# Reading the moving operand of 256-column products alternately from its two halves, in a hybrid encoder layer on one core

## The chip, the core and the metric

The kernel runs on one core of one Trainium2 chip. The metric is the device time of one execution in microseconds (us). Three runs of the kernel before took 881.15, 881.81 and 883.31 us, so its median is 881.81 us.

## The reference

One layer of a streaming encoder on x of 512 tokens by 1024 channels, all in float32:

```python
h = rms_norm(x, norm_mix)
proj = h @ w_in                      # 1024 -> 5*1024 + 3*1024
u_pool, u_lru, q, k, v, g_logits = split(proj)
gates = sigmoid(g_logits + b_gate)   # three gates of 1024 channels
y_pool = pool_mixer(u_pool)          # causal means over 2, 4, 8, 16 tokens, a 256x256 map per group
y_lru = rglru_mixer(u_lru)           # causal conv, two gates, a scan over tokens
y_sb = stick_breaking_attention(rms_norm(q), rms_norm(k), v)   # 8 heads of 128, causal
merged = sum(gates[b] * (y_b @ w_branch[b]) for b in range(3))
x = x + merged @ w_out
h2 = rms_norm(x, norm_ffn)
x = x + (silu(h2 @ w_ffn_gate) * (h2 @ w_ffn_up)) @ w_ffn_down   # 1024 -> 2816 -> 1024
```

## The kernel before, in words

Channels lie on the 128 partitions and tokens in the free dimension (512 of them), except for q, k and v, which are made with tokens on the partitions. To keep float32 accuracy on TensorE every operand is split into a high part of a reduced float32 type (`F32R`) and a low part that holds the rest: ScalarE (ACT) copies and rounds the high part, VectorE (DVE) subtracts to get the low part (`split_w`, lines 128 and 129, and `split_a`, lines 1425 and 1426). A product then takes three matmuls per block of k: high by high, high by low, low by high.

There are two kinds of products.

Products of 512 columns (`mm3`, lines 296 to 298, and lines 363, 721 and 818) stream all 512 tokens, or 512 weight columns. Their moving operand goes through `il`, which reads it alternately from its two halves: column 0, 256, 1, 257 and so on. Their results lie in PSUM in that order, and every reader undoes it with `in_order` (a step of two in PSUM) and `two` (the same shape of the unmixed tile). The attention products (z and py, also through `mm3`) do the same in blocks of 128 columns, of 64 and 64 (`b=64`); their widths are 128 x 4, 128 x 3 and 128 x 2.

Products of 256 columns come from the use of Strassen-like schemes: a 2 x 2 block product is made from seven products of sums of blocks instead of eight products, and each of the seven works on half of the tokens (`H` = 256 columns). One such product is 2 output blocks x 4 blocks of k x 3 matmuls, or 24 matmuls, each with its own load of 128 x 128 weights. There are four stages of them:

- the third branch's gate, two chunks of seven products (`product`, line 305; chunks at lines 873 to 901)
- the third branch's projection, 14 products in the order `BORDER` (line 1260)
- the feed-forward's gate and up projections, nine chunks of seven (`seven`, from line 1461, `product` again, line 305)
- the feed-forward's down projection, seven products of 20 blocks of k (`piece`, line 1633)

These read their moving operand straight through, 256 adjoining columns. Each product writes one half of a PSUM bank (`ps[:, w, half * H:(half + 1) * H]`). Partial sums are carried between banks by snapshots: after a product, ACT copies a half bank to SBUF (`act(t[:, :, ts_], src[:, :, ss], AF.Copy)`, lines 893, 1266 and 1477), and at the end of a chunk DVE adds the whole bank to it (`gate_done`, line 868; `merge7`, lines 1230 and 1232; `finish_act`, line 1452; `add`, line 1624, and line 1650 at the very end, which is followed by the store of the result).

The weights' split tiles rotate over three buffers each for high and low (`wp`). A buffer has room for 1024 + 128 elements, and a tile may begin at an offset in it. For the 256-column stages the first four products of a stage use offsets of 0, 4, 8 and 12 elements, and all later ones 16; all other weights begin at 0:

```python
OFF = 16
STEPS = (0, 4, 8, 12)
...
def weight_tiles(nh, nl, o=0):
    return [wp.tile([P, 1024 + 128], F32R, tag=tag, name=n)[:, o:o + 1024]
```

The order of the work on each engine is that of the program, with priorities (`tc.high_priority`) by which the splits of later weights are put ahead; background tasks are queued in `bg` and `abg` and called by `tick`. The weights come by DMA from the SP queue, and partly by adding DMAs from the GpSimd queue, which form the sums of blocks.

Of the kernel before, what the change touches and what calls it, by code (L numbers as in the profile page):

```python
# [32 lines left out]
H = S // 2  # L33
# [34 lines left out]
def layer_kernel(ctx: ExitStack, tc: tile.TileContext, x, xt, vecs, w_in, w_qkv7, w_gate7, w_pool, w_rg, w_ig,  # L68
# [38 lines left out]
    def two(ap, b=H):  # L107
        w = ap.ndim == 3
        if b == H:
            return ap.rearrange("p w (a b) -> p w a b" if w else "p (a b) -> p a b", b=b)  # L110
        return ap.rearrange("p (c a b) -> p c a b", a=2, b=b)

    def halves(t):
        return [t[:, 0:2, :], t[:, 2:4, :]]
# [185 lines left out]
    def product(a_, b_, ps, half, first, last, ws=(0, 1)):  # L300
        for w in ws:
            o = ps[:, w, half * H:(half + 1) * H]
            for k in range(4):
                for n, (a, b) in enumerate(((0, 0), (0, 1), (1, 0))):
                    nc.tensor.matmul(o, a_[a][:, w, k, :], b_[b][:, k, :],  # L305
                                     start=first and n == k == 0,
                                     stop=last and n == 2 and k == 3, skip_group_check=True)

# [117 lines left out]
    with ExitStack() as first:  # L426
# [438 lines left out]


        def gate_done(cc, j, t, ps):
            dve.tensor_tensor(t, t, ps, ALU.add)
            for w in range(2):
                act(t[:, w, :], t[:, w, :], AF.Sigmoid, scale=-1.0 if j else 1.0,  # L870
                    bias=vcol("b_gate", 16 + 2 * (2 * cc + w) + j))
            nc.gpsimd.dma_start(gd2[cc, j], t)

        for cc in range(2):
            tx, ty = b4([2, S], f"gx{cc}"), b4([2, S], f"gy{cc}")
            if cc:

                dve.memset(pb.tile([P, 2, S], F32, tag="mm", name="skip_g")[:, 0, 0:1], 0.0)
            Y = pb.tile([P, 2, S], F32, tag="mm", name=f"ps_gy{cc}")
            X = pb.tile([P, 2, S], F32, tag="mm", name=f"ps_gx{cc}")  # L880
            lo, hi = slice(0, H), slice(H, S)
            plan = {"11": (Y, 1, True, tx, lo, Y, hi),
                    "12": (X, 0, True, None, None, None, None),
                    "S2": (Y, 1, False, tx, hi, Y, hi),
                    "S1": (X, 1, False, ty, hi, X, hi),
                    "S3": (Y, 1, False, ty, lo, Y, hi),
                    "S4": (X, 1, False, None, None, None, None),
                    "22": (Y, 0, False, None, None, None, None)}
            for nm in ORDER:
                ps, half, first_, t, ts_, src, ss = plan[nm]  # L890
                product(weights("seven", 3 + cc, nm, 0), BQ[WITH[nm]], ps, half, first_, True)
                if t is not None:
                    act(t[:, :, ts_], src[:, :, ss], AF.Copy)
                if nm == "S4":
                    gate_done(cc, 0, tx, X)
                if nm == "22":
                    gate_done(cc, 1, ty, Y)
                tick(2)
                if (cc, nm) == (1, "12"):
                    q_scales()  # L900
# [305 lines left out]
    with ExitStack() as third:  # L1206
        ap2 = third.enter_context(tc.tile_pool(name="ap2", bufs=4, reuse_waits="tile"))
        bg.extend([lambda n=n: third_part(n) for n in range(4)] + [lambda n=n: fourth_part(n) for n in range(4)])
        gts = {}
        for u in range(2):  # L1210
            for i in range(2):
                gts[u, i] = ap2.tile([P, 2, S], F32, tag="g", name=f"g2{u}{i}")
                for j in range(2):
                    nc.sync.dma_start(gts[u, i][:, j, :], gd2[u, j][:, i, :])

        lo, hi = slice(0, H), slice(H, S)

        plan = {"11": ("Y", 1, True, 0, lo), "12": ("X", 0, False, None, None),
                "S1": ("X", 1, True, 1, hi), "S2": ("Y", 1, False, 0, hi),
                "S3": ("Y", 1, False, 1, lo), "S4": ("X", 1, False, None, None),  # L1220
                "22": ("Y", 0, False, None, None)}
        bank, snaps = {}, {}

        def merge7(u, i, ps):
            t, g, c = snaps[u, i], gts[u, i], 2 * u + i
            m = pairs[c]
            with tc.high_priority(60):
                if (u, i) in gated:
                    t = g
                    dve.tensor_tensor(t, g, ps, ALU.mult)  # L1230
                else:
                    dve.tensor_tensor(t, t, ps, ALU.add)
                    dve.tensor_tensor(t, t, g, ALU.mult)
                dve.tensor_tensor(m, m, t, ALU.subtract if i else ALU.add)
            h, l = corner([2, S], f"mth{c}", F32R), corner([2, S], f"mtl{c}", F32R)
            act(h, m, AF.Copy)
            dve.tensor_tensor(l, m, h.bitcast(F32), ALU.subtract)
            for j in range(2):
                mt[2 * c + j] = h[:, j, :], l[:, j, :]


        gated = [(0, 0), (0, 1), (1, 0)]

        def gate7(u, i):
            t, m = snaps[u, i], pairs[2 * u + i]
            dve.tensor_tensor(t, t, gts[u, i], ALU.mult)
            nc.gpsimd.dma_start(m, t, accum_op=ALU.add)

        for u, nm in BORDER:
            z, half, first_, sn, ts_ = plan[nm]  # L1250
            if (u, z) not in bank:
                bank[u, z] = fp.tile([P, 2, S], F32, tag="mm", name=f"ps_b{z}{u}")
            ps = bank[u, z]
            ah = weights("b7", u, nm)
            b = BH[nm]
            for w in range(2):
                o = ps[:, w, half * H:(half + 1) * H]
                for k in range(4):
                    for n, (x_, y_) in enumerate(((0, 0), (0, 1), (1, 0))):
                        nc.tensor.matmul(o, ah[x_][:, w, k, :], b[k][y_], start=first_ and n == k == 0,  # L1260
                                         stop=n == 2 and k == 3, skip_group_check=True)
            if sn is not None:
                if (u, sn) not in snaps:
                    snaps[u, sn] = ap2.tile([P, 2, S], F32, tag="t", name=f"bt{u}{sn}")
                with tc.high_priority(EARLY):
                    act(snaps[u, sn][:, :, ts_], ps[:, :, hi], AF.Copy,
                        scale=-1.0 if sn and (u, sn) in gated else 1.0)
            if nm in ("S2", "S3") and (u, sn) in gated:
                gate7(u, sn)
            tick()  # L1270
            if nm == "S4":
                merge7(u, 0, ps)
            if nm == "22":
                merge7(u, 1, ps)
# [3 lines left out]
    with ExitStack() as ffn:  # L1278
# [170 lines left out]

        def finish_act(t, ps, a):  # L1450

            dve.tensor_tensor(t, t, ps, ALU.add)
            act(t[:, 0, :], t[:, 0, :], AF.Silu)
            dve.tensor_tensor(a, t[:, 0, :], t[:, 1, :], ALU.mult)

# [3 lines left out]
        def seven(c):  # L1459
# [13 lines left out]
            for n, (nm, ps, half, first, t, ts_, src, ss) in enumerate(plan):  # L1473
                make_a(n0 + n + 3)
                product(A.pop((c, nm)), B[0, WITH[nm]], ps, half, first, True)
                if t is not None:
                    act(t[:, :, ts_], src[:, :, ss], AF.Copy)
                if c == DOWN - 1 and nm in PRE:
                    split_d2("11", PRE.index(nm), 0, 0)
                if nm == "S4":  # L1480
                    finish_act(tx, X, a[:, 0, :])
                if nm == "22":
                    finish_act(ty, Y, a[:, 1, :])
# [136 lines left out]
                "22": ("y", 0, True, [(1, lo, "y", lo)])}  # L1620

        def add(q, i, ts_, z, ss):
            t, ps = x1p[q, i][:, :, ts_], XY[q, z][:, :, ss]
            dve.tensor_tensor(t, t, ps, ALU.subtract if i else ALU.add)

        def piece(nm, q, use, ps, half, first, last, ws=(0, 1)):
            n, kh, k0, nk = use
            a_, b_ = DA[nm, n], DB[nm, kh]
            for w in ws:
                o = ps[:, w, half * H:(half + 1) * H]  # L1630
                for k in range(nk):
                    for i, (a, b) in enumerate(((0, 0), (0, 1), (1, 0))):
                        nc.tensor.matmul(o, a_[a][:, w, k0 + k, :], b_[b][:, k, :],  # L1633
                                         start=first and i == k == 0,
                                         stop=last and i == 2 and k == nk - 1, skip_group_check=True)

        for nm in DORDER:
# [3 lines left out]
            for q in range(2):  # L1641
                if (nm, q) == ("22", 1):

                    make_d(len(dsets))
                    for w, ps in enumerate((XY[1, "y"], XY[0, "x"])):
                        ws = slice(w, w + 1)
                        for p_, use in enumerate(USE[q]):
                            piece(nm, q, use, ps, half, first and p_ == 0, p_ == 2, (w,))
                        t = x1p[q, 1][:, ws, lo]
                        dve.tensor_tensor(t, t, ps[:, ws, lo], ALU.subtract)  # L1650
                        store(q, 1, lo, ws)
                    continue
                for p_, use in enumerate(USE[q]):
# [60 lines left out]
```

## Time and profile before

| | us |
|---|---|
| median of three runs | 881.81 |
| the profiled execution | 882.75 |
| its span, first to last instruction | 881.0 |
| TensorE matmul (PE) busy | 868.6 |
| TensorE weight load (PEld) busy | 798.1 |
| VectorE (DVE) busy | 740.9 |
| ScalarE (ACT) busy | 525.7 |
| GpSimd (POOL) busy | 90.9 |

The profile is that of one execution. Its span is a little shorter than the device time. An engine's busy time counts each moment once, though matmuls overlap: each is shown from its start to its modelled end, and the next starts before that. So the pace of PE is read from the starts, not from the durations. A row of a group gives line, engine, operation, what it writes and reads, shapes and count, then busy us and mean ns of one, then the idle time before it and what ended that. A row of the timeline gives start, duration, and in brackets the idle time before and its cause. The chain of work that ended last is followed back from the last instruction, at each step to what released it or to the instruction before it on its engine.

### The profile page before, as it was taken

The numbers are of one execution on the slowest core, as the hardware profiler recorded it, in microseconds if no ns is written. First come the engines' busy times: TensorE is split into PE (matmuls) and PEld (weight loads), VectorE is DVE, ScalarE is ACT, GpSimd is POOL, SyncE is SP. The second block draws the span as 40 slices with busy tenths as digits, with TensorE's granted clock in tenths as the row PEclk, the third lists the DMA queues.
The fourth block names the chain that finished last, engine by engine and source line by source line (L and its number), as shares of the span: only waits on it lengthen the run. The fifth ranks groups of instructions, "written<-read, shape, count | busy, mean of one in ns | idle before, by whom it ended". The sixth has DMA issues, their size and how long they took to land.

```text
span 881.0 us, 14269 instructions
## 1 busy us (share of the span) xinstructions
PE 868.6 (99%) x5563; PEld 798.1 (91%) x5563; DVE 740.9 (84%) x958; ACT 525.7 (60%) x730; POOL 90.9 (10%) x130
## 2 busy tenths in 40 slices
PE   9999989999999999999999999999999999999998
PEld 7888878888899888889889998889999999999998
DVE  7899787998786599977898786699988888899974
ACT  7555979556956556565664545464555555755642
POOL 1110002132433101000001100000000000121200
PEclk9999999999999999999999999999999999999999
DMA  9596346798592786735727855344533433798913
GB/s 338 151 306 187 96 159 174 200 330 259 179 277 72 226 252 198 221 121 154 230 84 171 188 168 175 103 141 134 163 99 96 119 99 119 225 238 204 188 31 120
DMA packets 116643, 154.08 MB, mean 175 GB/s; under 512 B 8160, under 2 KB 90080, under 8 KB 116576
## 3 DMA queue, kind: packets, MB, share of 16 engines
q1 hardware_dynamic: 103904, 107.30, 38.3%
q0 software_dynamic: 12528, 45.62, 21.7%
q8 instruction: 43, 0.70, 0.3%
q10 hardware_dynamic: 144, 0.26, 0.1%
q14 instruction: 24, 0.20, 0.1%
HBM read 132.71 MB, written 18.87 MB: 172 GB/s over the span
## 4 chain that ended last, share of the span: by engine, by line
PE 78%; DVE 11%; ACT 6%; DMA 2%; issue 2%; SPq 1%; ACTq 0%; DVEq 0%
PE ps_y L305 10%; PE ps_x L305 8%; PE ps_q L818 7%; PE ps_dy L1633 6%; PE ps_dx L1633 5%; DVE wlo L129 3%; PE ps_br L296 3%; PE ps_br L297 3%; PE ps_br L298 3%; PE ps_bY L1260 3%; PE ps_gate L721 2%; PE ps_gy L305 2%; PE ps_bX L1260 2%; PE ps_gx L305 2%; ACT whi L128 1%
## 5 line engine op out<-in xcount | busy, mean ns | idle before, releaser
L128 ACT ACTIVATE whi<-raw 128x1024 fp32r<-128x1024 f32 x69 | 72.8, 1055 | 80.1 <-PE ps_out L297 16.1
L129 DVE TENSOR_TENSOR wlo<-raw,whi 128x1024 fp32r<-128x1024 f32 x69 | 84.4, 1223 | 23.5 <-ACT whi L128 22.9
L129 DVE TENSOR_TENSOR wlo<-qw,whi 128x1024 fp32r<-128x1024 f32 x48 | 58.5, 1222 | 19.1 <-ACT whi L128 19.0
L128 ACT ACTIVATE whi<-qw 128x1024 fp32r<-128x1024 f32 x48 | 50.5, 1053 | 29.8 <-PE ps_q L818 14.8
L1425 ACT ACTIVATE wh_S<-w_S 128x1024 fp32r<-128x1024 f32 x36 | 38.2, 1065 | 34.9 <-PE ps_y L305 20.8
L1537 POOL DMA_DIRECT2D dw<-in_w_down_dram x20 | 16.9, 862 | 310.1 <-DMA dw<-in_w_down_dram 251.1
L1426 DVE TENSOR_TENSOR wl_S<-w_S,wh_S 128x1024 fp32r<-128x1024 f32 x36 | 43.8, 1222 | 4.5 <-ACT wh_S L1425 4.4
L1425 ACT ACTIVATE wh<-w 128x1024 fp32r<-128x1024 f32 x27 | 28.7, 1065 | 27.9 <-issue 9.3
L1426 DVE TENSOR_TENSOR wl<-w,wh 128x1024 fp32r<-128x1024 f32 x27 | 33.0, 1222 | 9.8 <-ACT wh L1425 9.8
L1425 ACT ACTIVATE whdS<-dw 128x1024 fp32r<-128x1024 f32 x20 | 21.3, 1065 | 22.5 <-PE ps_dy L1633 11.0
L1426 DVE TENSOR_TENSOR wldS<-dw,whdS 128x1024 fp32r<-128x1024 f32 x20 | 24.3, 1223 | 6.5 <-ACT whdS L1425 6.4
L1076 DVE TENSOR_TENSOR_SCAN E<-K,ahead 128x512 f32<-128x512 f32 (+3 forms) x32 | 25.4, 815 | 3.9 <-ACT K L1072 3.9
L298 PE MATMUL ps_gate<-HH,wlo 128*128 128x512 f32 x64 | 25.0, 390 | 2.2 <-DVE wlo L129 2.2
L296 PE MATMUL ps_br<-yHH,whi 128*128 128x512 f32 x64 | 24.6, 385 | 1.4 <-ACT up L963 1.4
L296 PE MATMUL ps_gate<-HH,whi 128*128 128x512 f32 x64 | 25.1, 392 | 0.0
L297 PE MATMUL ps_gate<-HL,whi 128*128 128x512 f32 x64 | 24.9, 389 | 0.0
L296 PE MATMUL ps_lru<-HH,whi 128*128 128x512 f32 x64 | 24.6, 384 | 0.0
L296 PE MATMUL ps_br<-yph,whi 128*128 128x512 f32 x64 | 24.5, 383 | 0.0
L296 PE MATMUL ps_pool<-HH,whi 128*128 128x512 f32 x64 | 24.5, 383 | 0.0
L297 PE MATMUL ps_lru<-HL,whi 128*128 128x512 f32 x64 | 24.3, 379 | 0.0
L298 PE MATMUL ps_lru<-HH,wlo 128*128 128x512 f32 x64 | 24.3, 379 | 0.0
L297 PE MATMUL ps_pool<-HL,whi 128*128 128x512 f32 x64 | 24.3, 379 | 0.0
(737 smaller groups left out, 3441.2 us busy)
## 6 DMA issues: line engine op xcount, KB each, us to landing
raw<-in_w_in_dram SPq DMA_DIRECT2D x31, 512.0 KB, 5.3
qw<-in_w_qkv_dram SPq DMA_DIRECT2D x24, 512.0 KB, 7.1
dw<-in_w_down_dram POOLq DMA_DIRECT2D x20, 512.0 KB, 7.4
w<-in_w_ffn_gate_dram SPq DMA_DIRECT2D x36, 256.0 KB, 3.5
w<-in_w_ffn_up_dram SPq DMA_DIRECT2D x36, 256.0 KB, 4.3
raw<-in_w_branch_dram SPq DMA_DIRECT2D x16, 512.0 KB, 4.0
qw<-in_w_qkv_dram POOLq DMA_DIRECT2D x12, 512.0 KB, 8.1
qd<-r POOLq DMA_DIRECT2D x12, 512.0 KB, 7.5
```

The source lines that it names most:

```text
L128: act(hi, raw, AF.Copy)
L129: dve.tensor_tensor(lo, raw, hi.bitcast(F32), ALU.subtract)
L296: nc.tensor.matmul(ps, lh, rh, start=start, stop=False, skip_group_check=skip)
L297: nc.tensor.matmul(ps, lh, rl, start=False, stop=False, skip_group_check=skip)
L298: nc.tensor.matmul(ps, ll, rh, start=False, stop=stop, skip_group_check=skip)
L305: nc.tensor.matmul(o, a_[a][:, w, k, :], b_[b][:, k, :], start=first and n == k == 0, stop=last and n == 2 and k == 3, skip_group_check=True)
L818: nc.tensor.matmul(ps[:, a, :], b_[:, k, ts_], il(a_[:, kk, :]), start=first and n == k == 0, stop=n == 2 and k == 3, skip_group_check=True)
L1076: dve.tensor_tensor_scan(E[:, c0:c0 + n][:, ::-1], K[:, c0 + 1:c0 + n + 1][:, ::-1], ahead[:, S - n:][:, ::-1], 0.0, ALU.mult, ALU.add)
L1260: nc.tensor.matmul(o, ah[x_][:, w, k, :], b[k][y_], start=first_ and n == k == 0, stop=n == 2 and k == 3, skip_group_check=True)
L1425: act(h, src, AF.Copy)
L1426: dve.tensor_tensor(l, src, h.bitcast(F32), ALU.subtract)
L1633: nc.tensor.matmul(o, a_[a][:, w, k0 + k, :], b_[b][:, k, :], start=first and i == k == 0, stop=last and i == 2 and k == nk - 1, skip_grou ...
```

## The change

The moving operand of the 256-column products goes through a new helper `il2`, which reads columns 0, 128, 1, 129 and so on. The bank's half then holds the tokens in that order, so all readers of these banks get `in_order2` on the PSUM side, a step of two inside each half, and `two2` on the SBUF side. The number of instructions, their sizes, the buffers, the offsets of the weights and the DMAs stay as they are.

```diff
+    def il2(ap):
+        return ap.rearrange("p (a b) -> p b a", a=2)
+
+    def in_order2(ap):
+        if ap.shape[-1] == H:
+            return ap.rearrange("p w (b a) -> p w a b", a=2)
+        return ap.rearrange("p w (c b a) -> p (w c) a b", c=2, a=2)
+
+    def two2(ap):
+        if ap.shape[-1] == H:
+            return ap.rearrange("p w (a b) -> p w a b", a=2)
+        return ap.rearrange("p w (c a b) -> p (w c) a b", c=2, a=2)
...
-                    nc.tensor.matmul(o, a_[a][:, w, k, :], b_[b][:, k, :],
+                    nc.tensor.matmul(o, a_[a][:, w, k, :], il2(b_[b][:, k, :]),
...
-            dve.tensor_tensor(t, t, ps, ALU.add)
+            v = two2(t)
+            dve.tensor_tensor(v, v, in_order2(ps), ALU.add)
...
-                    act(t[:, :, ts_], src[:, :, ss], AF.Copy)
+                    act(two2(t[:, :, ts_]), in_order2(src[:, :, ss]), AF.Copy)
...
-                        nc.tensor.matmul(o, ah[x_][:, w, k, :], b[k][y_], start=first_ and n == k == 0,
+                        nc.tensor.matmul(o, ah[x_][:, w, k, :], il2(b[k][y_]), start=first_ and n == k == 0,
...
-            t, ps = x1p[q, i][:, :, ts_], XY[q, z][:, :, ss]
+            t, ps = two2(x1p[q, i][:, :, ts_]), in_order2(XY[q, z][:, :, ss])
...
-                        nc.tensor.matmul(o, a_[a][:, w, k0 + k, :], b_[b][:, k, :],
+                        nc.tensor.matmul(o, a_[a][:, w, k0 + k, :], il2(b_[b][:, k, :]),
```

The first matmul of the diff is that of `product`, the second that of the branch products and the third that of `piece`. The other readers (`merge7`, `finish_act`, the snapshot at line 1266 and the last adds) change in the same way.

More of the change, by code (lines that the diff above doesn't have):

```diff
@@ L1229, in merge7 @@
                     t = g
-                    dve.tensor_tensor(t, g, ps, ALU.mult)
+                    dve.tensor_tensor(two2(t), two2(g), in_order2(ps), ALU.mult)
                 else:
-                    dve.tensor_tensor(t, t, ps, ALU.add)
+                    dve.tensor_tensor(two2(t), two2(t), in_order2(ps), ALU.add)
                     dve.tensor_tensor(t, t, g, ALU.mult)
@@ L1265, in layer_kernel @@
                 with tc.high_priority(EARLY):
-                    act(snaps[u, sn][:, :, ts_], ps[:, :, hi], AF.Copy,
+                    act(two2(snaps[u, sn][:, :, ts_]), in_order2(ps[:, :, hi]), AF.Copy,
                         scale=-1.0 if sn and (u, sn) in gated else 1.0)
@@ L1450, in finish_act @@
         def finish_act(t, ps, a):
-            dve.tensor_tensor(t, t, ps, ALU.add)
+            v = two2(t)
+            dve.tensor_tensor(v, v, in_order2(ps), ALU.add)
             act(t[:, 0, :], t[:, 0, :], AF.Silu)
@@ L1476, in seven @@
                 if t is not None:
-                    act(t[:, :, ts_], src[:, :, ss], AF.Copy)
+                    act(two2(t[:, :, ts_]), in_order2(src[:, :, ss]), AF.Copy)
                 if c == DOWN - 1 and nm in PRE:
@@ L1648, in layer_kernel @@
                             piece(nm, q, use, ps, half, first and p_ == 0, p_ == 2, (w,))
-                        t = x1p[q, 1][:, ws, lo]
-                        dve.tensor_tensor(t, t, ps[:, ws, lo], ALU.subtract)
+                        t = two2(x1p[q, 1][:, ws, lo])
+                        dve.tensor_tensor(t, t, in_order2(ps[:, ws, lo]), ALU.subtract)
                         store(q, 1, lo, ws)
```

## The prediction

> **What bounds the kernel now.** First the head of the page and its chain of work that ended last.
>
> ```profile
> span 881.0 us, 14269 instructions
> ...
> PE 868.6 (99%) x5563; PEld 798.1 (91%) x5563; DVE 740.9 (84%) x958; ACT 525.7 (60%) x730; POOL 90.9 (10%) x130
> ...
> PE 78%; DVE 11%; ACT 6%; DMA 2%; issue 2%; SPq 1%; ACTq 0%; DVEq 0%
> PE ps_y L305 10%; PE ps_x L305 8%; PE ps_q L818 7%; PE ps_dy L1633 6%; PE ps_dx L1633 5%; DVE wlo L129 3%; PE ps_br L296 3%; PE ps_br L297 3%; PE ps_br L298 3%; PE ps_bY L1260 3%; PE ps_gate L721 2%; PE ps_gy L305 2%; PE ps_bX L1260 2%; PE ps_gx L305 2%; ACT whi L128 1%
> ```
>
> PE is busy for 868.6 of 881.0 us, and three of the lines that carry its chain, 305, 1260 and 1633, are exactly those that the change edits. So the question is how fast PE starts one matmul after another in them. Durations can't say that: a matmul of 256 columns is shown with 277 ns and its successor starts long before its end. The chain in order of time gives it, since it merges the 24 matmuls of one product (columns: start, us, engine and line, count).
>
> ```profile
> 254.72 2.87 PE ps_gy L305 x24
> 257.59 2.84 PE ps_gx L305 x24
> 260.44 2.84 PE ps_gy L305 x24
> 263.27 2.83 PE ps_gx L305 x24
> 266.10 2.72 PE ps_gy L305 x24
> ...
> 476.21 2.88 PE ps_bY L1260 x24
> 479.09 5.68 PE ps_bX L1260 x48
> 484.77 2.83 PE ps_bY L1260 x24
> ...
> 782.11 14.09 PE ps_dy L1633 x120
> 796.21 27.20 PE ps_dx L1633 x240
> ```
>
> The usual product takes 2.72 us (27.20 / 10), or 113.3 ns per matmul. The first four of a stage take 2.87, 2.84, 2.84 and 2.83, together 11.38. What differs in those four is one thing in the code: their weight tiles begin 0, 4, 8 and 12 elements into the buffer (`STEPS`), all later ones 16 (`OFF`). The same pattern stands at 476 (2.88 + 5.68 + 2.83 = 11.39) and at 782 (14.09 - 2.72 = 11.37). So the pace depends on where the weights lie against a moving operand that is read straight through: the two reads get in each other's way.
>
> **What an alternate read does in this kernel already.** The attention products (lines 296 to 298 on z and py) have matmuls of 256 columns whose moving operand is read alternately, from places 64 columns apart. Three runs of them, each with its second and its last row of nine (columns: start, duration).
>
> ```profile
> 343.43 0.28 PE L297 MATMUL py<-wtl,vh 128*128 128x256 f32 x1
> ...
> 344.21 0.28 PE L298 MATMUL z<-qkh,qkl 128*128 128x256 f32 x1
> ```
>
> ```profile
> 366.26 0.28 PE L297 MATMUL py<-wtl,vh 128*128 128x256 f32 x1
> ...
> 367.04 0.28 PE L298 MATMUL z<-qkh,qkl 128*128 128x256 f32 x1
> ```
>
> ```profile
> 456.71 0.28 PE L297 MATMUL py<-wtl,vh 128*128 128x256 f32 x1
> ...
> 457.50 0.28 PE L298 MATMUL z<-qkh,qkl 128*128 128x256 f32 x1
> ```
>
> Seven steps each: 0.78, 0.78 and 0.79 us, 2.35 / 21 = 111.9 ns, with rounding 111.4 to 112.4. That is the nearest row for the changed matmuls: the same columns, the same 128x128 weight load before each, an alternate read. I take 111.7, inside that rounding, so 2.68 us for a product of 24 against 2.72.
>
> The 512-column products are the second witness. They are read alternately from halves 256 columns apart; line 1333 alone reads 512 columns straight through.
>
> ```profile
> 561.62 0.38 PE L296 MATMUL ps_fg<-h2h,whi 128*128 128x512 f32 x1
> 561.84 0.38 PE L297 MATMUL ps_fg<-h2l,whi 128*128 128x512 f32 x1
> 562.31 0.49 PE L1333 MATMUL ps_rms<-sqh,onesr 128*128 128x512 f32 x1
> 562.64 0.38 PE L298 MATMUL ps_fg<-h2h,wlo 128*128 128x512 f32 x1
> ```
>
> ```profile
> 562.30 0.19 PEld L1333 LDWEIGHTS ps_rms<-sqh,onesr 128*128 128x128 f32 x1 [0.49 <-ACT sqh L1330]
> 562.41 0.19 PEld L298 LDWEIGHTS ps_fg<-h2h,wlo 128*128 128x128 f32 x1
> ```
>
> Alternate matmuls of 512 follow at 0.22 us. Line 1333's own load began late; the next load could start 0.11 later (562.41), and from there to the next matmul it is 0.23. So the straight read seems to cost some 0.01 us there too, although the load beside it has time to spare. The pair of loads also shows the floor below which 256 columns can't go while every matmul has its own load: 0.11 us.
>
> **The change part by part.** Products: 7 in each of 2 gate chunks, 14 branch products, 7 in each of 9 feed-forward chunks, and 35 down products (7 by 20 blocks of k, each 2 x 3 matmuls, is 840 matmuls), in all 14 + 14 + 63 + 35 = 126 products or 3024 matmuls of the page's 5563. Sixteen are first-fours of the four stages, 110 the usual kind.
>
> - Usual products: 110 x (2.72 - 2.68) = 4.4 us gone.
> - First-fours, if the clash of the straight read goes whatever the shift: 4 x (11.38 - 4 x 2.68) = 4 x 0.66 = 2.6 us gone.
> - Given back: in the feed-forward's first four PE already waits.
>
> ```profile
> 608.39 0.39 PE L305 MATMUL ps_x<-B0T1h,wl_S 128*128 128x256 f32 x1 [0.67 <-DVE wl_S L1426]
> ```
>
> DVE's split of the weights ends that wait. Three products before it get shorter by 0.16 each and lengthen the wait instead: 0.5 us lost again.
>
> - The weights' supply elsewhere: PE's gain is kept only if ACT and DVE keep up.
>
> ```profile
> 611.10:770.10 159.00, 159.00 (x1405) 159.00 (x1404) 140.49 (x130) 93.17 (x116) 1.73 (x3) 1.00 0.45 130
> ```
>
> In the longest stretch (columns: window, length, PE, PEld, DVE, ACT, POOL, clock, DMA share, GB/s) DVE works 140.5 of 159.0 us. At 2.68 a product the stretch shrinks to 156.7, so the cover holds. The granted clock is 1.00 already; nothing comes from there.
>
> - PSUM readers with a step of two: rows of both kinds exist.
>
> ```profile
> L1477 ACT ACTIVATE ty<-ps_y 128x512 f32<-128x512 f32 x9 | 5.2, 581 | 0.0
> L1104 ACT ACTIVATE ysb<-py 128x512 f32<-128x512 f32 x8 | 4.7, 592 | 5.2 <-PE py L298 5.2
> L963 ACT ACTIVATE up<-ps_pool 128x512 f32<-128x512 f32 x8 | 4.4, 609 | 0.0
> ```
>
> ```profile
> L1452 DVE TENSOR_TENSOR tx<-tx,ps_x 128x1024 f32<-128x1024 f32 x9 | 11.0, 1221 | 3.8 <-PE ps_x L305 3.8
> L835 DVE TENSOR_TENSOR r<-r,ps_q 128x1024 f32<-128x1024 f32 x9 | 11.0, 1219 | 0.7 <-PE ps_q L818 0.6
> ```
>
> Line 1477 reads in order, 1104 and 963 with a step: +11 to +28 ns on ACT; on DVE 1219 (step) against 1221 (in order). ACT has 93 of 159 us of work in the stretch above, and a snapshot has a whole product of 2.7 us before the bank that it reads is written again. I cost them at nothing; with no cover, 52 snapshots would be 0.6 to 1.5 us. No DMA, queue, load or matmul is added or moved, and no wait.
>
> Sum: 4.4 + 2.6 - 0.5 = 6.5 us. The profiled execution took 882.75 us, 1.75 around its span of 881.0, and lies 0.94 above the median of 881.81. So 882.75 - 6.5 = 876.2 for it, and 881.81 - 6.5 = **875.3 us** as the forecast.
>
> Two rules of the Trainium skill bear on this. Its page "SBUF — State Buffer", in "Door 1: The DMA port swizzle", says that SBUF is read in lines of 16 bytes and that each access that crosses to a new line pays; by that, reading from two halves in turn, a new line at each element, makes the stream slower. The rows of 512 columns at 0.22 us, read alternately, speak against it. Its page "TensorE: Matmul & The Clock Gate", in "Step-by-step: what each phase is for", says that the moving operand and the weights come through independent ports and that loading takes nothing from a running matmul; by that neither the shift of the weights nor the order of reading would matter, and the sum would be 0. The 2.87 against 2.72 us between products that differ in the shift alone speaks against it.
>
> **The rivals.**
>
> A, the forecast: the new read runs at the pace of the attention rows. For it: 21 measured steps, and no alternate row that is slower. Against it: those rows' weights aren't shifted by 16 elements, and their places are 64 or 256 columns apart, not 128. Own range 2.67 to 2.70 a product: 874 to 878 us.
>
> B, slower: a new clash. The alternate read walks each half at half pace, nearer to that of a weight load (128 elements in the 0.11 us in which 256 are streamed), so with the shift of 16 the two could stay side by side for the whole load instead of passing once. That shift may fit the straight read alone. For it: no row has an alternate 256-column read with shifted weights, and a shift of 16 is worth 0.15 us a product now. Against it: the unshifted alternate rows show no clash. Its price by the nearest row, the worst product seen, 2.87: 110 x 0.15 + 4 x (11.48 - 11.38) = 16.9, so 898.7 us. It decides from 2.74 a product on: there 110 x 0.02 uses up what the first-fours bring (2.6 - 0.5). If alternation itself costs at this distance, as the rule on lines would have it, the price from rows is the same, with a chance of 0.02 inside this rival.
>
> C, nothing: the usual 113.3 ns come from PE's own step and not from the reads; then only the first-fours can fall to 2.72, 4 x 0.50 - 0.3 = 1.7 us: 880.1, or all stays at 881.8. For it: 113.3 and 111.9 are close. Against: 24 equal matmuls at both paces, and the dependence on the shift.
>
> D, more: the load alone is the floor, 0.11 us (109 ns if the rounding is kind): 2.62 a product, 110 x 0.10 + 4 x 0.90 - 0.7 = 13.9: 867.9 us. Against: the attention rows have the same loads and stay near 112.
>
> **How the numbers follow.** A 0.65, B 0.19, C 0.11, D 0.05. A measurement of this kernel tells about 0.3%, 2.6 us, from no change. Faster by more than that: A but for its edge, and D, 0.68; within: C and A's edge, 0.13; slower: 0.19. The range leaves out most of B and little else: from 868.0 (D) to 886.0 (a mild B, 2.755 a product, 110 x 0.035 + 0.3 = 4.2 us worse).
>
> **What would show it.** In the chain by time: products of lines 305, 1260 and 1633 at 2.68 where they were 2.72, and no difference left between a stage's first four and the rest. PE's wait at line 305 for the split grows from 0.67 to about 1.2. ACT's snapshots rise to 590 to 610, DVE's adds stay at 1220. I am wrong if the usual products show 2.74 or more (B), if they stay at 2.72 (C), or if they fall and PE gets new waits for DVE or DMA that give it back.

## The result, and the profile after

The changed kernel took 874.46 us (median of four runs, 873.78 to 875.54), the kernel before 882.56 us beside it (four runs). The ratio is 0.9911, with an interval of 0.9892 to 0.9930, or 6.2 to 9.5 us less. The forecast was 875.3 us and 6.5 us less. Line numbers are now 318, 1274 and 1648 for the changed matmuls (305, 1260 and 1633 before).

The page after, its span and its first row:

```profile
span 872.0 us, 14269 instructions
...
PE 859.1 (99%) x5563; PEld 789.4 (91%) x5563; DVE 740.8 (85%) x958; ACT 525.4 (60%) x730; POOL 90.8 (10%) x130
```

DVE, ACT and POOL have the same work as before to 0.3 us; only PE and its loads got shorter. The chain in order of time says where (start, us, engine and line, count of matmuls):

```profile
252.55 2.68 PE ps_gy L318 x24
255.23 2.68 PE ps_gx L318 x24
257.91 2.68 PE ps_gy L318 x24
260.59 2.68 PE ps_gx L318 x24
263.27 2.72 PE ps_gy L318 x24
...
472.76 2.68 PE ps_bY L1274 x24
...
775.04 13.40 PE ps_dy L1648 x120
788.44 26.80 PE ps_dx L1648 x240
```

A product takes 2.68 us where it took 2.72, and the first four of a stage, with weights at 0, 4, 8 and 12 elements, are no longer slower than the rest: 2.68 where they took 2.83 to 2.88.

The two profiled spans differ by 9.0 us, more than the 8.1 us between the medians. The first changed product begins at 252.55 instead of 254.72: 2.2 us were gone before any changed matmul ran. One window of each profile shows why (window, length, busy PE, PEld, DVE, ACT and POOL, granted clock, DMA share, GB/s). Before:

```profile
119.00:123.00 4.00, 4.00 (x12) 3.16 (x12) 4.00 (x5) 1.60 (x3) 0.76 (x1) 0.57 0.72 197
```

After:

```profile
119.00:123.00 4.00, 4.00 (x21) 3.24 (x19) 4.00 (x4) 1.27 (x3) 0.76 (x1) 1.00 0.81 225
```

In the execution of before that was profiled, the granted clock fell to 0.57 in these 4 us and PE got through 12 matmuls instead of 21. Nothing of the change lies there; 9.0 - 2.2 = 6.8 us are left for it and for what followed from it. The clock shows in other runs too. Of 22 further runs of the kernel before, taken beside the later kernels, those with a mean granted clock of 1.0 took 880.07 to 881.04 us, but for two of 887, and those with 0.997 or 0.998 took 881.97 to 884.29. The changed kernel took 873.78 and 873.96 at 1.0, 874.95 at 0.999 and 875.54 at 0.998. Compared at 1.0 the difference is 6.1 to 7.3 us, the two of 887 left aside. So the 8.1 us between the medians probably hold some luck of the clock; what clock the four runs of the kernel before had isn't on record.

### The profile page after: what moved, and what is told of

Its sections match the earlier page's. It is cut to its first block, busy times and chain, and to the rows that moved or that the text cites. A ratio compares the mean times of both kernels' runs of the same rounds, so it can differ in the third digit from the quotient of the medians.

```text
span 872.0 us, 14269 instructions
## 1 busy us (share of the span) xinstructions
PE 859.1 (99%) x5563; PEld 789.4 (91%) x5563; DVE 740.8 (85%) x958; ACT 525.4 (60%) x730; POOL 90.8 (10%) x130
## 4 chain that ended last, share of the span: by engine, by line
PE 77%; DVE 11%; ACT 6%; DMA 3%; issue 2%; SPq 0%; ACTq 0%; DVEq 0%
PE ps_y L318 10%; PE ps_x L318 8%; PE ps_q L831 7%; PE ps_dy L1648 6%; PE ps_dx L1648 5%; DVE wlo L142 3%; PE ps_br L309 3%; PE ps_br L310 3%; PE ps_br L311 3%; PE ps_bY L1274 2%; PE ps_gate L734 2%; PE ps_gy L318 2%; PE ps_bX L1274 2%; PE ps_gx L318 2%; ACT whi L141 2%
```

## The experiments

The theory: a moving operand that is read straight through and the load of the next weights hinder each other; the alternate read doesn't hinder the load, and then the load alone sets the pace. Rivals: the alternate read is free only at some places of the weights (a clash of its own); the 113.3 ns are PE's own step; the readers of PSUM make part of the difference. Twelve kernels were run, the first five of them several times and the others once. The pace of a product is read from one row of each kernel's chain, ten products of the down stage, unless another row is shown.

**The alternate read with another shift of the weights.**

```diff
-OFF = 16
-STEPS = (0, 4, 8, 12)
+OFF = 64
+STEPS = ()
```

> The changed kernel with all weights of its 256-column products shifted by 64 elements from the first product on, instead of 0, 4, 8, 12 and then 16. Clash theory (a straight moving read and the weight load beside it get in each other's way, an alternate read does not): still 2.68 us a product everywhere, 874.5 us, the same as the changed kernel within 0.3%. Rival, the alternate read is free only at certain shifts: some products at 2.75 to 2.87, 883 to 897 us.

```profile
788.90 26.80 PE ps_dx L1648 x240
```

2.68 us a product, 875.54 us, ratio to before 0.9919 (0.9890 to 0.9948). With the first four products of the changed kernel these are six shifts, 0, 4, 8, 12, 16 and 64, all at 2.68. The rival of a new clash falls.

**The straight read with other shifts.** Four places were tried, each with `STEPS = ()` in the kernel before and `OFF` as named. Shift 0:

> The kernel before with no shift of the weights in any 256-column product. Clash theory: every product becomes like the first of a stage before, 2.87 us; 110 x 0.15 us more and 16 first-fours 0.1 us more in all, 899 us. Rival, the usual 113.3 ns are PE's own step and the slow first four are a start effect of the stage: 2.72 after the first four of each stage, 882.6 us.

```profile
807.76 28.80 PE ps_dx L1633 x240
```

Shift 64:

> The kernel before with all weights of the 256-column products shifted by 64 elements from the first product on. Clash theory, if the clash repeats only over a longer distance than 64 elements: 2.72 or less in every product, the first four too, so 882.6 - 1.5 = 881 us, at best 2.68 and 876 us. If it repeats with 64 elements: 2.87 everywhere, 899 us. Rival, start effect: the first four stay at 2.84 and the rest at 2.72, 882.6 us.

```profile
807.35 28.80 PE ps_dx L1633 x240
```

Shift 32:

> The kernel before with all weights of the 256-column products shifted by 32 elements. The straight read was at 2.88 us a product with shifts of 0 and of 64 and at 2.72 with 16. If the clash repeats with 32 elements or less: 2.88, 899 us. If it repeats with 64 alone: 2.72 or another value below 2.88.

```profile
806.28 28.48 PE ps_dx L1633 x240
```

Shift 24:

> As before, with a shift of 24 elements. If there is a shift at which a straight read is as good as the alternate one, 2.68 us and 874.5 us; if 16 is the middle of the good places, between 2.72 and 2.85; if the clash repeats with 8 elements, 2.88.

```profile
805.13 28.48 PE ps_dx L1633 x240
```

Shift 0: 2.88 us a product to the end of the stage, 900.39 us, ratio 1.0198 (1.0165 to 1.0232). So the slow first four were no start effect; and since the alternate read is at 111.7 ns in the same products, 113.3 ns is no step of PE's own. Both rivals fall. Shift 64: 2.88 and 898.50 us, ratio 1.0185 (1.0149 to 1.0221); the hope that a shift beyond 16 would do as well was wrong. Shifts 32 and 24: 2.85 (one run each, 896.65 and 895.51 us). With a shift of 24 the gate and the branch stage are a little faster than the two others; two rows of the branch stage:

```profile
476.66 2.82 PE ps_bY L1260 x24
479.48 5.63 PE ps_bX L1260 x48
```

So the shift of the weights isn't all that counts; what else differs between the stages wasn't followed up. Of the places tried, 16 is the best by far and still stays at 2.72; none reaches what the alternate read has everywhere.

**The two parts of the change alone.** First the readers' step of two, with `il2` returning its operand as it is:

> The changed kernel with the straight read back in the matmuls, and the readers' step of two kept, so the tokens in each half are mixed up. Clash theory, readers cost nothing: as the kernel before, 882.6 us within 0.3%, products at 2.87 to 2.83 and then 2.72. Rival, the readers make part of the difference: more than 2.6 us off 882.6 in either direction, with other durations of the snapshots or the adds.

```profile
794.61 27.20 PE ps_dx L1648 x240
```

Then the alternate read, with `in_order2` and `two2` returning their operands as they are:

> The changed kernel with its readers back to reading PSUM in order, so the tokens in each half stay mixed up; the matmuls read alternately as in the change. Clash theory, all of the gain is in the matmuls: 2.68 us a product, 874.5 us within 0.3%. Rival, readers matter: further than 2.6 us from 874.5.

```profile
819.17 26.80 PE ps_dy L1644 x240
```

Readers alone: 883.27 us, ratio 1.0012 (0.9983 to 1.0042), products as before; three of its ten runs took 889 us, for a reason that isn't known. The read alone: 875.82 us, ratio 0.9926 (0.9910 to 0.9943), products at 2.68. All of the gain is in the matmuls.

**How far apart the two places must be.** Both kernels have the readers in order. Four columns apart, with the shifts of the changed kernel:

```diff
     def il2(ap):
-        return ap.rearrange("p (a b) -> p b a", a=2)
+        return ap.rearrange("p (c a b) -> p c b a", a=2, b=4)
```

> As the kernel with the alternate read alone, but the two places are 4 columns apart (0, 4, 1, 5, 2, 6, 3, 7, 8, 12 ...), so the read as a whole goes straight on at full pace through the 256 columns; tokens are mixed up. If what helps is that each place moves on at half pace over a long stretch: no help, 2.72 us with the shift of 16, and 2.83 to 2.87 in the first four, 882 us. If what helps is alternation as such, at any distance: 2.68 us, 874.5 us. If switching places so near costs by itself: above 2.87.

```profile
790.36 26.80 PE ps_dx L1644 x240
```

Two columns apart (`b=2`) and no shift:

> As the kernel that reads from two places 4 columns apart, but 2 columns apart (0, 2, 1, 3, 4, 6, 5, 7 ...), and without any shift of the weights; tokens are mixed up. With 4 apart it was 2.68 us a product. If what helps is that neighbouring reads fall on different stretches of 16 bytes (4 columns) or more: no help here, 2.88 us and 899 us. If they only need to differ by 8 bytes, or the order as such helps: 2.68 us and 875 us.

```profile
808.83 28.80 PE ps_dx L1644 x240
```

Four apart is as good as 128 apart: 2.68, 875.71 us. Two apart doesn't help at all: 2.88, 900.19 us, the pace of the straight read at the same shift. The missing shift isn't the reason, since the first product of a stage has no shift in the kernel with four apart either:

```profile
474.71 2.68 PE ps_bY L1270 x24
```

So what counts isn't that each place walks on slowly, as rival B of the prediction had pictured the pair of streams; it is how far neighbouring reads lie apart: 8 bytes (two columns of 4 bytes) are too few and 16 are enough. That neighbours must not fall within one stretch of 16 bytes fits both, but no run shows that it is such a stretch. One run each, but the products are at one value or the other throughout.

**Is it the load?** The straight read without shift, with half a load in the second matmul of each block of k:

```diff
-nc.tensor.matmul(o, a_[a][:, w, k, :], ...
+nc.tensor.matmul(o[0:64] if n == 1 else o, a_[a][:, w, k, 0:64 if n == 1 else P], ...
```

> The kernel before without any shift, and with 64 instead of 128 weight columns in the second matmul per block of k, whose part is left out for half of the channels. Clash theory: the step in which the half load runs (from the first matmul to the second) is shorter than the other two, which stay at 118 to 120 ns, since a load of half the length is beside the straight read for half the time; near 113 or less. Rival, the clash isn't with the load: all three steps alike, 118 to 120.

```profile
829.88 28.00 PE ps_dy L1633 x240
```

The same with the changed kernel:

> The changed kernel, but the second of the three matmuls per block of k loads and uses 64 weight columns instead of 128; that part of the high-by-low products is left out for half of the channels. If the 111.7 ns that are left are the time of a whole load beside the matmul: the step in which the half load runs (from the first matmul to the second) falls to about 109 ns or less, and the other two stay at 111.7; products at 2.66 or less. If 111.7 is the time of streaming 256 columns: all three stay at 111.7, 2.68 us a product.

```profile
816.85 26.60 PE ps_dy L1648 x240
```

One load of three halved takes a sixth of the loading away. The straight read falls from 2.88 to 2.80 (890.81 us), the alternate one from 2.68 to 2.66 (874.99 us), so the excess of the straight read over the alternate one falls from 0.20 to 0.14 us a product: the clash shrinks with the load, though by more than a sixth. These are one run each, the halved matmul also writes only half of the partitions, and no run takes a load away whole. That the load takes part rests as much on the shifts above, which move nothing but the weights.

The expectations named the step from the first to the second matmul as the short one, and that was wrong for both. In the trace's nanoseconds the steps of the alternate kernel, from the first to the second, to the third and to the next first, are 111 to 112, 109 to 110 and 111 to 112. The short step is the one behind the matmul whose own weights, half a load, were there early. The attention rows of the kernel before have the same: the step behind the matmul at 343.32, whose load ran beside a matmul of 384 columns, is 109, and those after it are 111 to 112. In the straight kernel the three steps average 116.0, 115.4 and 118.6 over the feed-forward products from 620 us on, where all are 120 with whole loads; two of them are short, not one.

**What sets the 111.7 ns that are left?** The changed kernel, with 192 columns streamed in the second matmul:

```diff
+z = slice(0, 192 if n == 1 else H)
-nc.tensor.matmul(o, a_[a][:, w, k, :], il2(b_[b][:, k, :]), ...
+nc.tensor.matmul(o[:, z], a_[a][:, w, k, :], il2(b_[b][:, k, z]), ...
```

> The changed kernel, but the second of the three matmuls per block of k streams 192 columns instead of 256; that part of the high-by-low products is left out for 64 tokens. If the load sets what is left: no step falls by the 27 ns that a quarter of 107 ns of streaming is worth, all stay at 109 to 112 ns, products at 2.64 to 2.68. If streaming sets it: one step in three falls to 80 to 90 ns, products at 2.45 to 2.5.

Its matmuls (start, duration) and its loads over one block of k and a little more:

```profile
640.04 0.28 PE L319 MATMUL ps_x<-B022h,wh_S 128*128 128x256 f32 x1
640.15 0.25 PE L319 MATMUL ps_x<-B022l,wh_S 128*128 128x192 f32 x1
640.24 0.30 PE L319 MATMUL ps_x<-B022h,wl_S 128*128 128x256 f32 x1
640.38 0.28 PE L319 MATMUL ps_x<-B022h,wh_S 128*128 128x256 f32 x1
```

```profile
640.04 0.19 PEld L319 LDWEIGHTS ps_x<-B022l,wh_S 128*128 128x128 f32 x1
640.16 0.19 PEld L319 LDWEIGHTS ps_x<-B022h,wl_S 128*128 128x128 f32 x1
640.27 0.19 PEld L319 LDWEIGHTS ps_x<-B022h,wh_S 128*128 128x128 f32 x1
640.38 0.19 PEld L319 LDWEIGHTS ps_x<-B022l,wh_S 128*128 128x128 f32 x1
```

And its products in the same stretch:

```profile
637.19 2.68 PE ps_y L319 x24
639.87 2.68 PE ps_x L319 x24
```

One matmul does start early after the short one (0.09 instead of 0.11), as the rival had it, but the next waits the longer (0.14), and the block of k takes 0.34 as before. The loads go on at 0.11 to 0.12 each, unmoved by the shorter stream. So the load sets the pace, by little: with weights there early a step took 109 ns, as above. The expectation that no step falls was wrong; that the product stays at 2.68 was right, and the rival's 2.45 to 2.5 didn't come. The run as a whole took 888.6 us, with waits of PE elsewhere that the other kernels don't have, the longest of 4.6 us for a snapshot in the branch stage. Why they came wasn't followed up, and its time isn't used.

## Why the prediction was right, point by point

- **The pace of a product**: right. 2.68 was taken from the attention rows, and 2.68 came in all four stages, but for one product at 2.72 and a few beside a wait or at the end of a stage. The choice of the nearest row, with the same columns and the same load, carried the forecast. The second witness is described wrongly in one point: line 1333 isn't alone in reading 512 columns straight through, line 1334 does so too. Nothing in the sum rests on it.
- **The first fours**: right, 2.68 each. That they were slow through the place of the weights, read from the 2.87 and 2.72 of before, is confirmed by the straight read at shift 0.
- **What is given back**: right. PE's wait for the split in the feed-forward's first four was to grow from 0.67 to 1.2 us. In the changed kernel it stands at 0.77, with another of 0.16 ahead of it. The stage's first matmul is shown with it:

```profile
594.22 0.27 PE L318 MATMUL ps_y<-B011h,wh 128*128 128x256 f32 x1
...
602.58 0.38 PE L318 MATMUL ps_x<-B0T1h,wh_S 128*128 128x256 f32 x1 [0.16 <-ACT wh_S L1439]
...
603.84 0.38 PE L318 MATMUL ps_x<-B0T1h,wl_S 128*128 128x256 f32 x1 [0.77 <-DVE wl_S L1440]
```

  The first matmul of this stage before:

```profile
598.77 0.28 PE L305 MATMUL ps_y<-B011h,wh 128*128 128x256 f32 x1
```

  The brackets add up to 0.93, only 0.26 more than 0.67, but they count idle time from the modelled end of the matmul ahead, and each new wait hides part of itself there. The starts tell it better: from the stage's first matmul to the one behind the long wait it is 9.62 us in both kernels (608.39 - 598.77 and 603.84 - 594.22). All that the products in between gained, 3 x 0.16 = 0.5 us, went into the waits.
- **The cover by DVE and ACT**: right. In the longest stretch DVE works 140.9 of 157.0 us:

```profile
607.10:764.10 157.00, 157.00 (x1409) 157.00 (x1408) 140.94 (x131) 93.13 (x117) 2.56 (x3) 1.00 0.46 133
```

- **The readers**: cost nothing, as forecast, and less than the bounds. Snapshots were to rise to 590 to 610 ns:

```profile
L1492 ACT ACTIVATE ty<-ps_y 128x512 f32<-128x512 f32 x9 | 5.2, 578 | 0.0
...
L907 ACT ACTIVATE gy<-ps_gx 128x512 f32<-128x512 f32 x2 | 1.2, 594 | 0.0
```

```profile
L1467 DVE TENSOR_TENSOR tx<-tx,ps_x 128x1024 f32<-128x1024 f32 x9 | 11.0, 1220 | 3.4 <-PE ps_x L318 3.3
```

  They stay at 578 to 594, and the adds at 1220. The 592 and 609 of the rows that were compared must have another reason than the step of two; which one isn't known.
- **A whole product of cover for each snapshot**: not always. In the gate stage of some executions PE waits for one; the kernel with the alternate read alone has the wait below (us in total, times, longest). It may also be what lengthened the one product of 2.72 in the changed kernel. It isn't a price of the alternate read: with the straight read at a shift of 24 the same product, the fifth of the stage, took 3.08 us where its neighbours took 2.81 and 2.82.

```profile
PE ps_gy L314 <- ACT gx L903: 0.6, 1, 0.6
```

- **The sum**: right. 6.5 us stands inside the measured 6.2 to 9.5, and the profiles have 6.8 once the 2.2 us of the clock are taken off. The 0.3 us between them lie where the change does nothing. From the first product of the gate stage to that of the branch stage the kernel became 1.3 us faster (221.49 to 220.21), of which its 14 products bring 1.0. Part of the rest is a wait for a DMA in the attention, which of the two profiled executions only that of before has:

```profile
PE pq L1039 <- DMA at<-qd: 0.2, 1, 0.2
```

- **The rivals**: B, a new clash, is refuted at six shifts; C, nothing, by the pace; D, the lower floor, by the load, which sets 111.7 and not 109. The two rules of the Trainium skill don't hold here. That reads which stay in one line of 16 bytes are the fast ones ("SBUF — State Buffer", "Door 1: The DMA port swizzle") is turned round beside a weight load: with unshifted weights, reads two columns apart, whose four neighbours take up 16 bytes, give 2.88 us a product, and reads four columns apart 2.68. That a load takes nothing from a running matmul ("TensorE: Matmul & The Clock Gate", "Step-by-step: what each phase is for") fails on the straight read, which takes 2.88 us with its weights at 0 and 2.72 with its weights at 16.

## What to carry to other kernels

Where PE is dense, read its pace from the starts of matmuls and compare products that differ in one thing only: here the first four of a stage told of a clash that no wait and no busy time shows. A wait, too, is better read from starts than from brackets, which hide what lies under a modelled end. Float32 operands of one matmul and the next one's load can be kept out of each other's way by the order in which the moving operand is read; here it cost nothing to let the readers of PSUM undo it, and it works at any place of the weights that was tried, while a shift of the weights helps much at one place only. Once the clash is gone, matmuls of 256 columns with a load each are bound by the load, so faster streaming alone brings nothing. Less loading alone can by estimate bring no more than 111.7 - 109 = 2.7 ns a matmul, or 8 us for the 3024 of these stages, since about 109 ns is the shortest step that a matmul of 256 columns showed. Beyond that both have to shrink.

## What the runs showed that was not expected

- Alternation over four columns is enough (2.68 us a product) and over two is worth nothing (2.88). Why a shift of 16 elements is good for the straight read (2.72) and 24, 32 and 64 are not (2.82 to 2.85, 2.85, 2.88) stays open: no run tells how the memory is divided.
- Halving one load of three took 0.06 us of the 0.20 us of clash, more than its share of a sixth.
- The granted clock can fall for some 4 us behind a wait of PE for `wlo` that ends at 118 us: to 0.57 in the profiled execution of before, behind a wait of 2.22 us, and not at all (1.00) in that of after, behind one of 2.21. Why it falls in some executions only stays open. It moves a span by 2 us, a third of what this change gave, so two profiles alone would have misstated the gain.
